# A two-layer decoder trunk on one core: the first products of each stage in a fixed order, the statistics product at tile 1, the Silu table loaded behind the affines

## The chip, the cores and the metric

The kernel runs on one core of one Trainium2 chip. A core has a tensor engine (PE in the profile, with its weight loads as PEld), a vector engine (DVE), a scalar engine (ACT), GpSimd (POOL) and a sync engine (SP) that issues most transfers. Each engine takes its instructions in the order in which they stand in its own queue; between engines they wait for semaphores. Products are summed in PSUM, in banks of 128 partitions by 512 columns; all other data lies in SBUF. The metric is device time in microseconds, the median of several runs. Times inside a profile count from the first instruction.

## The reference

One sequence of 512 positions with 1024 channels runs through two layers. Layer 0 mixes tokens with stick-breaking attention, layer 1 with a diagonal state-space layer; behind each mixer stands a gated feed-forward stage with a causal convolution of width 3. Each of these four stages starts with a root-mean-square norm that a conditioning vector scales and shifts. Cut to what matters here:

```python
def rms_norm(x, g):
    xf = x.astype(jnp.float32)
    y = xf * lax.rsqrt(jnp.mean(xf * xf, axis=-1, keepdims=True) + EPS)
    return (y * g.astype(jnp.float32)).astype(x.dtype)

def modulate(h, shift, scale):
    return h * (1 + scale[:, None, :]) + shift[:, None, :]

def conv_ffn(h, w_up, conv_w, conv_b, w_down):
    up = h @ w_up
    up = lax.conv_general_dilated(
        up, conv_w[:, None, :], window_strides=(1,), padding=[(CONV_W - 1, 0)],
        dimension_numbers=('NWC', 'WIO', 'NWC'), feature_group_count=2 * D_FF) + conv_b
    gate, val = jnp.split(up, 2, axis=-1)
    return (jax.nn.silu(gate) * val) @ w_down

# in reference(), for each layer i
        x = x + g1[:, None, :] * y
        h = modulate(rms_norm(x, norm_ffn[i]), sh2, sc2)
        x = x + g2[:, None, :] * conv_ffn(h, w_up[i], conv_w[i], conv_b[i], w_down[i])
```

## The kernel before

**Layout and precision.** Activations lie with channels on partitions: `x` is eight tiles of 128 channels by 512 positions, and so is the normed `h`. Every operand of a product is split into a high and a low part, made by ACT (the rounded copy) and DVE (the difference): `hH`, `hL` for `h`, and names ending in `_h`, `_l` for weights. A product of one weight tile and one tile of `h` is then three: high by high, high weight by low `h`, low weight by high `h`. The function `mm3` (L170 to L177) issues them in this order. Eight tiles make one output of 128 channels by 512 positions in one PSUM bank.

**Heads.** A stage's *head* is its first four outputs, computed while the norm in front of the stage is still being made: `head_mm` (L324 to L345) in both feed-forward stages (products `up`, of units 0 and 1, each a gate and a value) and in the state-space layer (products `u`, four of eight). The norm's statistics come in two halves of 256 positions. The first half's product stands in the stage before; the second half's is issued inside the head by `rstd_stat`, at a place that `HEADS` gives. Its result lets `norm_tile` (L304 on) make the second half of `h`: for each tile one multiplication on DVE (`nt`), two affines on ACT (`hH`, and `nt` again in place of a full-precision copy), one subtraction on DVE (`hL`). The head goes through tiles 0 to 5 for the first 256 positions, tiles 0 to 5 for the second 256, and tiles 6 and 7 for all 512, and multiplies each tile with all four weights.

**What sets the order.** A scheduler orders each engine's queue by its own estimate of times. `pe_pin` keeps an instruction in the order of the program, and `behind_head` and `follow` issue one behind given others. In the head before, only some products are pinned: those of tile 0 and the statistics product. The rest is left to the scheduler, which may put products of the next unit among them.

**Buffers.** PSUM's main pool has six banks, handed out in turn. In a feed-forward stage the head holds four of them and unit 2 the next two. In layer 0 the result `gm` of the gate of units 2 and up takes a main bank as well (units 0 and 1 use another pool), and unit 3 follows. Split weights go round in five buffers of each kind (`NW`), raw weights in three; two of the head's four weights lie in such buffers and two in their own. The loop over `HEADW` issues the loads and splits of the next five weights (the products of units 2 and 3 and the first of unit 4), each behind a given tile's affines.

**Behind the head.** `unit_out` (L467 on) takes a unit out of PSUM: `conv` evicts with ACT (`ca`, L462) and adds two taps on DVE (L464), ACT makes Silu of the gate (L474), DVE multiplies gate and value (`gm`), ACT and DVE split the result into `gH` and `gL`. The first Silu needs another function table on ACT than the norm before it, so an ACT_TABLE_LOAD stands there. In layer 0, DVE, ACT and POOL also prepare tables for the state-space layer in between (L1020 to L1078 and others). In the state-space layer `u_out` (L1297 to L1300) copies a finished `u` to memory and reads it back in another layout; the first block's products `pv` (L1291) wait for it.

Of the kernel before, what the change touches and what calls it, by code (L numbers as in the profile page):

```python
# [8 lines left out]
F32 = mybir.dt.float32  # L9
# [3 lines left out]
AF = mybir.ActivationFunctionType  # L13
# [4 lines left out]
P = 128  # L18
T = 512
D = 1024  # L20
KD = D // P
# [11 lines left out]
STATK = 0  # L33
STATN = 2
HEADK = 6
HEADS = (1, 2)
HEADW = (4, 8, 11, 13, 13)
UPRE = 12
NACC = 6
NIDLE = (5, 2, 0, 9, 0)  # L40
# [48 lines left out]
def _trunk(ctx, tc, I, out, tap):  # L89
# [15 lines left out]
    def pe_pin(ins):  # L105
        tc.keep_in_program_order(ins)
# [64 lines left out]
    def mm3(ps, lhs, rhs, start, stop, pinned=False):  # L171
        (ah, al), (bh, bl) = lhs, rhs
        ins = PE.matmul(ps, ah, bh, start=start, stop=False)  # L173
        if pinned:
            tc.keep_in_program_order(ins)
        PE.matmul(ps, ah, bl, start=False, stop=False)  # L176
        PE.matmul(ps, al, bh, start=False, stop=stop)  # L177
# [148 lines left out]
    def head_mm(R, h, a, b, hd):  # L326
        pin["head"] = []
        todo = [(k, HALF[0]) for k in range(HEADK)] + [(k, HALF[1]) for k in range(HEADK)] + [(k, FULL) for k in range(HEADK, KD)]
        made = 0
        for n, (k, cr) in enumerate(todo):  # L330

            while made < (min(n + 3, HEADK) if cr == HALF[0] else n + 1):
                norm_tile(h, todo[made][0], R["bc"], a, b, todo[made][1])
                made += 1
            for q, (w, ps) in enumerate(hd):
                if cr == HALF[0] and (k, q) == HEADS:
                    rstd_stat(R, HALF[1], True)
                if n:
                    mm3(ps[:, cr], wk(w, k), (h[0][k][:, cr], h[1][k][:, cr]), k == 0 and cr.start == 0, k == KD - 1)
                else:  # L340
                    for half in range(2):
                        pe_pin(PE.matmul(ps[:, cr], wk(w, k)[half], h[0][k][:, cr], start=not half, stop=False))
            if not n:
                for w, ps in hd:
                    pe_pin(PE.matmul(ps[:, cr], wk(w, k)[0], h[1][k][:, cr], start=False, stop=False))  # L345

    @contextmanager
    def behind_head(pins=None):
# [80 lines left out]
    def ffn(l, R, prep=None, last=None, hook=lambda: None):  # L429
# [4 lines left out]
        with ExitStack() as fc:  # L434
# [61 lines left out]
            for gi, gn in enumerate(GROUPS):  # L496
                gs = []
                i = i0
                if gi == 2:
                    hook()  # L500
                if gi == 0:
                    hx, ws = pin["hw"]
                    hd = [(q, s, ws[2 * q + s], bank(name=f"up{l}_{q}_{s}")) for q in range(2) for s in range(2)]
                    head_mm(R, h, a, b, [q[2:] for q in hd])
                    hx.close()
                    for q in range(len(HEADW)):
                        with behind_head(pin["head"][HEADW[q]]):
                            split_next(q > 2)
                    if not l:
                        bg(2, False, hold=behind_head)  # L510
                    pin["prep"] = [pin["split"]]
                    for q in range(2):
                        gs.append(unit_out(q, q, [hd[2 * q + s][3] for s in range(2)]))
                    i = 2
                    step = prep(fc) if prep else (lambda: None)
                for i in range(i, i0 + gn):
                    av = []
                    for s in range(2):
                        w, ps = take(), bank(name=f"up{l}_{i}_{s}")
                        for k in range(KD):  # L520
                            mm3(ps, wk(w, k), (h[0][k], h[1][k]), k == 0, k == KD - 1)
                        av.append(ps)
                    skip = [i == 2]

                    def nxt():
                        if not skip or not skip.pop():
                            split_next()

                    gs.append(unit_out(i, i - i0, av, nxt))
                    if l or (4, 0, 0)[gi] <= i - i0 < (8, 2, 6)[gi]:  # L530
                        bg(BGU if l else 1, lined=True)
                    pace(11.0)

                def after():
                    if l == 0 and gi < 2:
                        bg(1, lined=True)
                    pace(5.4)

                head = None
                if gi == 2 and prep:  # L540
                    while step():
                        pass
                    head = [I["w_in"][bi * P:(bi + 1) * P, :] for bi in range(4)], "win"
                R2 = out_proj(lambda mt: I["w_down"][(l * KD + mt) * P:(l * KD + mt + 1) * P, i0 * P:(i0 + gn) * P], gs, mcol(l, 5, 0),
                         acc2 if gi == 2 else None, f"dn{l}_{gi}_", tail=TAIL + (FINT if last else 0), n=gn * P, after=after, last=last if gi == 2 else None, head=head,
                         getw=lambda mt: take(), step=split_next)
                i0 += gn
# [956 lines left out]
    R = ssm(R)  # L1504
# [156 lines left out]
```

## Time and profile before

| | |
|---|---|
| Median of 3 runs | 1162.76 us (1162.4 to 1164.23) |
| The profiled execution | 1162.41 us |
| Its span, first to last instruction | 1160.6 us |
| Mean granted TensorE clock | 0.997 |
| Head of layer 0's feed-forward stage | from 252.90 us |
| Head of the state-space layer | from 626.1 us |
| Head of layer 1's feed-forward stage | from 789.0 us |

Busy shares are of the span. The span in 40 slices, with the busy share of each engine in tenths:

```profile
PE   9999999999999999999999999999999999999997
DVE  7869989576998577687867598787598378744655
ACT  7656577455552244313347477547443144422443
POOL 1001110000589799879800000000000000000003
PEclk9999999999999999999999999999999999999999
```

PE is busy in every slice. The other lines that carry the argument stand in the prediction. A row of a timeline reads: start, duration, engine, line of the kernel, operation, what it writes and reads, sizes and count; in brackets stand idle time of the engine before it and what ended that.

### The profile page before, as it was taken

How to read it: one execution, taken by the hardware profiler on the slowest of the kernel's cores; microseconds unless marked ns; L12 is line 12 of the kernel's file. 1: busy time of each engine (PE TensorE's matmuls, PEld its weight loads, DVE VectorE, ACT ScalarE, POOL GpSimd, SP SyncE). 2: the span in 40 equal slices, each digit the busy share in tenths (PEclk: the TensorE clock that was granted, in tenths of full speed). 3: DMA queues.
4: the chain of work that ended last, by engine and by line, in shares of the span. 5: the costliest groups of instructions: out<-in, count | busy, mean ns of one | idle time of the engine just before them, and what ended most of it. 6: DMA issues, size and time to landing. Idle time of an engine off the chain costs nothing.

```text
span 1160.6 us, 16497 instructions
## 1 busy us (share of the span) xinstructions
PE 1149.5 (99%) x6212; PEld 960.4 (83%) x6212; DVE 854.4 (74%) x1273; ACT 563.1 (49%) x896; POOL 274.5 (24%) x279
## 2 busy tenths in 40 slices
PE   9999999999999999999999999999999999999997
PEld 7888777797888888888889888889888888888887
DVE  7869989576998577687867598787598378744655
ACT  7656577455552244313347477547443144422443
POOL 1001110000589799879800000000000000000003
PEclk9999999999999999999999999999999999999999
DMA  9875464323166668697766598461176357432222
GB/s 347 283 261 173 167 212 147 130 91 110 55 221 219 206 233 252 196 315 237 236 202 231 175 348 279 168 212 55 38 232 220 109 161 197 128 114 74 94 69 73
DMA packets 87777, 211.01 MB, mean 182 GB/s; under 512 B 15505, under 2 KB 33809, under 8 KB 87698
## 3 DMA queue, kind: packets, MB, share of 16 engines
q1 hardware_dynamic: 78994, 192.65, 50.6%
q0 software_dynamic: 4544, 16.26, 4.2%
q10 hardware_dynamic: 4160, 1.05, 0.4%
q8 instruction: 49, 0.80, 0.3%
q14 instruction: 30, 0.25, 0.1%
HBM read 188.68 MB, written 21.24 MB: 181 GB/s over the span
## 4 chain that ended last, share of the span: by engine, by line
PE 95%; DVE 2%; ACT 1%; POOL 1%; issue 1%; POOLq 0%; ACTq 0%
PE up L173 13%; PE up L177 13%; PE up L176 13%; PE dn L173 7%; PE dn L176 7%; PE dn L177 7%; PE o L838 2%; PE t L822 2%; PE glu L173 1%; PE wo L173 1%; PE py L1291 1%; PE u L173 1%; PE wo L176 1%; PE wo L177 1%; PE wos L177 1%; PE wos L176 1%
## 5 line engine op out<-in xcount | busy, mean ns | idle before, releaser
L173 PE MATMUL up<-hH,up_h 128*128 128x512 f32 x640 | 250.7, 392 | 2.4 <-DVE e L1028 2.4
L177 PE MATMUL up<-hH,up_l 128*128 128x512 f32 x640 | 249.8, 390 | 0.2 <-DVE up_l L168 0.2
L176 PE MATMUL up<-hL,up_h 128*128 128x512 f32 x640 | 249.9, 390 | 0.0
L464 DVE SCALAR_TENSOR_TENSOR ca<-up,small,ca 128x511 f32<-128x511 f32 (+1 forms) x176 | 131.5, 747 | 103.9 <-ACT ca L462 101.1
L173 PE MATMUL dn<-gH,dn_h 128*128 128x512 f32 (+1 forms) x394 | 144.5, 368 | 0.0
L176 PE MATMUL dn<-gL,dn_h 128*128 128x512 f32 (+1 forms) x394 | 144.5, 367 | 0.0
L177 PE MATMUL dn<-gH,dn_l 128*128 128x512 f32 (+1 forms) x394 | 144.4, 366 | 0.0
L173 PEld LDWEIGHTS up<-hH,up_h 128*128 128x128 f32 x640 | 120.4, 188 | 28.7 <-issue 3.6
L177 PEld LDWEIGHTS up<-hH,up_l 128*128 128x128 f32 x640 | 120.5, 188 | 25.7 <-DVE up_l L168 0.8
L176 PEld LDWEIGHTS up<-hL,up_h 128*128 128x128 f32 x640 | 120.6, 188 | 24.8
L168 DVE TENSOR_TENSOR up_l<-up_r,up_h 128x1024 fp32r<-128x1024 f32 x80 | 116.6, 1459 | 24.8 <-ACT up_h L167 20.9
L462 ACT ACTIVATE ca<-up,small 128x512 f32<-128x512 f32 x88 | 68.1, 774 | 132.9 <-PE up L177 132.9
L167 ACT ACTIVATE up_h<-up_r 128x1024 fp32r<-128x1024 f32 x80 | 84.0, 1053 | 93.8 <-PE dn L176 59.1
L204 DVE SCALAR_TENSOR_TENSOR wg<-wg,cact 128x1024 f32<-128x1024 f32 x96 | 120.7, 1276 | 6.0 <-DMA wg<-in_w_modT_dram 6.0
L1533 POOL TENSOR_SCALAR xa<-x,Anorm_out 128x256 f32<-128x256 f32 x7 | 5.7, 817 | 459.6 <-ACT dn_h L167 446.9
L360 DVE SCALAR_TENSOR_TENSOR x<-dn,mod,x 128x512 f32<-128x512 f32 (+1 forms) x55 | 37.4, 681 | 70.7 <-PE dn L177 70.3
L173 PEld LDWEIGHTS dn<-gH,dn_h 128*128 128x128 f32 x394 | 74.3, 189 | 12.8 <-issue 0.6
L177 PEld LDWEIGHTS dn<-gH,dn_l 128*128 128x128 f32 x394 | 74.3, 189 | 12.2
L176 PEld LDWEIGHTS dn<-gL,dn_h 128*128 128x128 f32 x394 | 74.3, 189 | 12.1
L167 ACT ACTIVATE dn_h<-dn_r 128x1024 fp32r<-128x1024 f32 (+1 forms) x48 | 46.5, 980 | 47.7 <-PE dn L176 37.7
L168 DVE TENSOR_TENSOR dn_l<-dn_r,dn_h 128x1024 fp32r<-128x1024 f32 (+1 forms) x48 | 59.6, 1242 | 0.7 <-ACT dn_h L167 0.5
L480 ACT ACTIVATE gH<-gm 128x512 fp32r<-128x512 f32 x44 | 27.1, 616 | 68.0 <-DVE gm L476 68.0
(370 smaller groups left out, 2297.0 us busy)
## 6 DMA issues: line engine op xcount, KB each, us to landing
up_r<-in_w_up_dram SPq DMA_DIRECT2D x80, 512.0 KB
wg<-in_w_modT_dram SPq DMA_DIRECT2D x74, 512.0 KB
dn_r<-in_w_down_dram SPq DMA_DIRECT2D x32, 512.0 KB
wg<-in_w_modT_dram POOLq DMA_DIRECT2D x22, 512.0 KB, 4.6
wgs<-in_w_modT_dram SPq DMA_DIRECT2D x16, 512.0 KB
dn_r<-in_w_down_dram SPq DMA_DIRECT2D x16, 384.0 KB
wv_r<-in_w_v_dram SPq DMA_DIRECT2D x8, 512.0 KB
wk_r<-in_w_qk_dram SPq DMA_DIRECT2D x8, 512.0 KB
```

The costliest lines, as they stand in the source:

```text
L167: order("S", lambda: S.activation(wh[:, :n], raw[:, :n], AF.Copy))
L168: pin["split"] = order("V", lambda: V.tensor_tensor(wl[:, :n], raw[:, :n], wh[:, :n].bitcast(F32), ALU.subtract))
L173: ins = PE.matmul(ps, ah, bh, start=start, stop=False)
L176: PE.matmul(ps, ah, bl, start=False, stop=False)
L177: PE.matmul(ps, al, bh, start=False, stop=stop)
L204: mul = lambda: V.scalar_tensor_tensor(w, w, 1.0, cact, ALU.mult, ALU.mult, accum_out=raw[:, col:col + 1])
L360: add = lambda: V.scalar_tensor_tensor(xs, pv, gate, xs, ALU.mult, ALU.add)
L462: follow("S", lambda: S.activation(ca, ps, AF.Identity, bias=small[:, cb:cb + 1], scale=tapw[2]))
L464: follow("V", lambda: V.scalar_tensor_tensor(ca[:, q:], ps[:, :T - q], tapw[2 - q], ca[:, q:], ALU.mult, ALU.add))
L480: follow("S", lambda: S.activation(gh, m, AF.Copy))
L822: pe_pin(PE.transpose(pt[:, c:c + P], wts[pr][h2][i][:, j * P:(j + 1) * P], ident))
L838: pe_pin(PE.matmul(po[pr][h2 * HD:(h2 + 1) * HD, j * P:], vn[:, j, hd:hd + HD], src, start=j == 0, stop=j == 3))
```

## The change

Four edits:

- In `head_mm`, all products are pinned, in a new order: for each tile first the products with its high part (high and low weight, for all four outputs), then those with its low part. What was left to the scheduler is now written out, so the next unit's products stand behind the head.
- `HEADS` is a tile: the second statistics product stands between the high and the low products of tile 1 in the first half. Before, it was ahead of output 2 of tile 1, and the scheduler moved it in the feed-forward stages, where the unpinned products came ahead of it or behind it.
- `HEADW` has four entries, so the loop splits four weights and not five, and none of them in the recorded order that `lined=True` gave the fourth and fifth. The fifth comes in `unit_out` of unit 2, where the call that was skipped before is now made. The first product of unit 2 is pinned.
- A one-column Silu (`warms`) is issued behind the last affines, so the table load stands there.

```diff
-HEADS = (1, 2)
-HEADW = (4, 8, 11, 13, 13)
+HEADS = 1
+HEADW = (4, 8, 11, 13)
...
-            for q, (w, ps) in enumerate(hd):
-                if cr == HALF[0] and (k, q) == HEADS:
-                    rstd_stat(R, HALF[1], True)
-                if n:
-                    mm3(ps[:, cr], wk(w, k), (h[0][k][:, cr], h[1][k][:, cr]), k == 0 and cr.start == 0, k == KD - 1)
-                else:
-                    for half in range(2):
-                        pe_pin(PE.matmul(ps[:, cr], wk(w, k)[half], h[0][k][:, cr], start=not half, stop=False))
-            if not n:
-                for w, ps in hd:
-                    pe_pin(PE.matmul(ps[:, cr], wk(w, k)[0], h[1][k][:, cr], start=False, stop=False))
+            def prod(ps, half, low):
+                return pe_pin(PE.matmul(ps[:, cr], wk(w, k)[half], h[low][k][:, cr], start=k == 0 and cr.start == 0 and half + low == 0, stop=k == KD - 1 and low == 1))
+
+            for w, ps in hd:
+                for half in range(2):
+                    prod(ps, half, 0)
+            if cr == HALF[0] and k == HEADS:
+                rstd_stat(R, HALF[1], True)
+            for w, ps in hd:
+                prod(ps, 0, 1)
...
-                            split_next(q > 2)
+                            split_next(False)
                     if not l:
                         bg(2, False, hold=behind_head)
+                    warm = np_.tile([P, 64], F32, tag="warm", bufs=1, name="warms")[:, 0:1]
+                    with behind_head():
+                        S.activation(warm, ones[:, 0:1], AF.Silu)
...
-                            mm3(ps, wk(w, k), (h[0][k], h[1][k]), k == 0, k == KD - 1)
+                            mm3(ps, wk(w, k), (h[0][k], h[1][k]), k == 0, k == KD - 1, i == 2 and not k)
                         av.append(ps)
-                    skip = [i == 2]
-
-                    def nxt():
-                        if not skip or not skip.pop():
-                            split_next()
-
-                    gs.append(unit_out(i, i - i0, av, nxt))
+                    gs.append(unit_out(i, i - i0, av, split_next))
```

How the queues change, at three places. The first is PE in the head of layer 0's feed-forward stage, where the second half of tile 0 begins. `up0_0_0` to `up0_1_1` are the four outputs of the head (layer, unit, gate or value), `upo0` to `upo3` their weights, `up0_2_0` the gate of unit 2. Before:

```order
L173 MATMUL up0_0_0_2586<-hH0_2566,upo0_h_2362 128x256
L173 MATMUL up0_0_1_2587<-hH0_2566,upo1_h_2368 128x256
L173 MATMUL up0_1_0_2588<-hH0_2566,upo2_h_2374 128x256
L173 MATMUL up0_1_1_2589<-hH0_2566,upo3_h_2380 128x256
L173 MATMUL up0_2_0_2918<-hH0_2566,up0_2_0_h_2850 128x512
L176 MATMUL up0_0_0_2586<-hL0_2574,upo0_h_2362 128x256
L177 MATMUL up0_0_0_2586<-hH0_2566,upo0_l_2363 128x256
L176 MATMUL up0_0_1_2587<-hL0_2574,upo1_h_2368 128x256
```

And in the changed kernel, from the same place in the queue:

```order
L336 MATMUL up0_0_0_2586<-hH0_2566,upo0_h_2362 128x256
L336 MATMUL up0_0_0_2586<-hH0_2566,upo0_l_2363 128x256
L336 MATMUL up0_0_1_2587<-hH0_2566,upo1_h_2368 128x256
L336 MATMUL up0_0_1_2587<-hH0_2566,upo1_l_2369 128x256
L336 MATMUL up0_1_0_2588<-hH0_2566,upo2_h_2374 128x256
L336 MATMUL up0_1_0_2588<-hH0_2566,upo2_l_2375 128x256
L336 MATMUL up0_1_1_2589<-hH0_2566,upo3_h_2380 128x256
L336 MATMUL up0_1_1_2589<-hH0_2566,upo3_l_2381 128x256
L336 MATMUL up0_0_0_2586<-hL0_2574,upo0_h_2362 128x256
L336 MATMUL up0_0_1_2587<-hL0_2574,upo1_h_2368 128x256
```

The product of unit 2, and 18 more like it in the rest of this head, now stand behind the head; the first product with the low part is the ninth, not the sixth. The statistics product, in the first half of the head, moves 20 products forward here and in layer 1; in the state-space layer it keeps its place.

The second place is ACT behind the affines of the same head: `ca0` is the eviction of a gate, `ca1` of a value, `up0_3_1_h` and `up0_4_0_h` are high parts of the fourth and the fifth weight. Before:

```order
L317 ACTIVATE nt2_2831<-nt1_2830,mod_110,Anorm_ffn0_2564 128x512
L167 ACTIVATE up0_3_1_h_2868<-up0_3_1_r_2867 128x1024
L167 ACTIVATE up0_4_0_h_2874<-up0_4_0_r_2873 128x1024
L462 ACTIVATE ca0_2885<-up0_0_0_2586,small_86 128x512
L474 ACT_TABLE_LOAD
L474 ACTIVATE gm_2889<-ca0_2885 128x512
L462 ACTIVATE ca1_2891<-up0_0_1_2587,small_86 128x512
L480 ACTIVATE gH0_2896<-gm_2889 128x512
```

In the changed kernel:

```order
L317 ACTIVATE nt2_2831<-nt1_2830,mod_110,Anorm_ffn0_2564 128x512
L512 ACT_TABLE_LOAD
L512 ACTIVATE warms_2879<-ones_103 128x1
L461 ACTIVATE ca0_2881<-up0_0_0_2586,small_86 128x512
L167 ACTIVATE up0_3_1_h_2868<-up0_3_1_r_2867 128x1024
L473 ACTIVATE gm_2885<-ca0_2881 128x512
L461 ACTIVATE ca1_2887<-up0_0_1_2587,small_86 128x512
L479 ACTIVATE gH0_2892<-gm_2885 128x512
L461 ACTIVATE ca0_2896<-up0_1_0_2588,small_86 128x512
L473 ACTIVATE gm_2900<-ca0_2896 128x512
L461 ACTIVATE ca1_2902<-up0_1_1_2589,small_86 128x512
L479 ACTIVATE gH1_2907<-gm_2900 128x512
```

The table load stands ahead of the first eviction, the fourth weight's split behind it, and the fifth's has gone further back, behind the eviction of unit 2's gate. DVE's halves of these splits move with them. In layer 1 the same happens.

The third place is PE at the end of the state-space layer's head: `u0` to `u3` are its outputs, `win0` to `win3` their weights. Before:

```order
L176 MATMUL u0_6046<-hL7_6015,win0_h_5831 128x512
L177 MATMUL u0_6046<-hH7_6007,win0_l_5832 128x512
L176 MATMUL u1_6047<-hL7_6015,win1_h_5837 128x512
L177 MATMUL u1_6047<-hH7_6007,win1_l_5838 128x512
L176 MATMUL u2_6048<-hL7_6015,win2_h_5843 128x512
L177 MATMUL u2_6048<-hH7_6007,win2_l_5844 128x512
L176 MATMUL u3_6049<-hL7_6015,win3_h_5849 128x512
L177 MATMUL u3_6049<-hH7_6007,win3_l_5850 128x512
```

In the changed kernel:

```order
L336 MATMUL u3_6051<-hH7_6009,win3_h_5851 128x512
L336 MATMUL u3_6051<-hH7_6009,win3_l_5852 128x512
L336 MATMUL u0_6048<-hL7_6017,win0_h_5833 128x512
L336 MATMUL u1_6049<-hL7_6017,win1_h_5839 128x512
L336 MATMUL u2_6050<-hL7_6017,win2_h_5845 128x512
L336 MATMUL u3_6051<-hL7_6017,win3_h_5851 128x512
```

The last product of `u0` is the fourth from the end, where it was the seventh. Besides, the scheduler moves three things by itself: in the state-space layer one load of a weight on SP's queue goes behind four other loads; in layer 1's first down group six products with the last slice come 21 products earlier; in layer 0 the table preparation on POOL and DVE is interleaved a little differently.

## The prediction

> **What bounds the kernel now.** I read the page's busy times first, then the list of who waited for whom on the tensor engine (PE), then the timeline at the one place where that list has something to give.
>
> ```profile
> span 1160.6 us, 16497 instructions
> PE 1149.5 (99%) x6212; PEld 960.4 (83%) x6212; DVE 854.4 (74%) x1273; ACT 563.1 (49%) x896; POOL 274.5 (24%) x279
> PE 95%; DVE 2%; ACT 1%; POOL 1%; issue 1%; POOLq 0%; ACTq 0%
> ...
> PE up L173 <- DVE e L1028: 2.4, 1, 2.4
> PE up L177 <- DVE up_l L168: 0.2, 1, 0.2
> ```
>
> PE is the path: 99% busy, and 95% of the chain that ended last. The last two rows are from its waits (us in total, times, longest). The change adds and removes no product, so it can gain only PE time that is not products at full speed, and it loses what PE must newly wait. Apart from the first 16 us, where the change does nothing, the list has one wait of 2.4 us and one of 0.2 us. PE's own timeline and its clock show what the larger one costs:
>
> ```profile
> 286.84 0.39 PE L177 MATMUL up<-hH,up_l 128*128 128x512 f32 x1
> 289.65 0.47 PE L173 MATMUL up<-hH,up_h 128*128 128x512 f32 x1 [2.43 <-DVE e L1028]
> ...
> 291.20 0.63 PE L173 MATMUL up<-hH,up_h 128*128 128x512 f32 x1
> 291.62 0.63 PE L176 MATMUL up<-hL,up_h 128*128 128x512 f32 x1
> ...
> 294.53 0.39 PE L177 MATMUL up<-hH,up_l 128*128 128x512 f32 x1
> 294.75 0.39 PE L173 MATMUL up<-hH,up_h 128*128 128x512 f32 x1
> ...
> 289.60:291.00 1.40, 1.35 (x6) 1.00 0.00 0
> 291.00:294.20 3.20, 3.20 (x10) 0.50 0.00 0
> ```
>
> The last two rows give stretches: PE's busy time, its instructions, then the granted clock. A 512-column product normally starts 0.22 to 0.23 us after the one before (294.53 to 294.75). After the wait, with the clock at 0.50, the step is 0.42 (291.20 to 291.62). From the product at 286.84 to that at 294.53 there are 15 steps; at 0.2275 they need 3.41 us, and they took 7.69. **The stall costs 4.28 us**: 2.6 for the wait, 1.7 for the clock behind it.
>
> Why PE waited: the six PSUM banks go round in the order of allocation. Unit 2's `gm` takes the bank of product (0, gate), so the first product of unit 3 takes that of (0, value), which comes free when the vector engine (DVE) has done its second tap. The scalar engine (ACT) and DVE came late there:
>
> ```profile
> 271.33 0.81 ACT L317 ACTIVATE nt<-nt,mod,Anorm_ffn 128x512 f32<-128x512 f32 x1
> 279.97 2.01 ACT L167 ACTIVATE up_h<-up_r 128x1024 fp32r<-128x1024 f32 x2 [7.82 <-PE up L176]
> 281.89 0.76 ACT L462 ACTIVATE ca<-up,small 128x512 f32<-128x512 f32 x1
> 285.35 1.28 ACT L474 ACT_TABLE_LOAD   x1 [2.70 <-DVE ca L464]
> 287.18 0.76 ACT L462 ACTIVATE ca<-up,small 128x512 f32<-128x512 f32 x1
> 298.38 0.78 ACT L462 ACTIVATE ca<-up,small 128x512 f32<-128x512 f32 x1
> ...
> 288.76 0.75 DVE L464 SCALAR_TENSOR_TENSOR ca<-up,small,ca 128x510 f32<-128x510 f32 x1
> ```
>
> ACT is done with h at 272.14, then stands 7.8 us before two weight splits that need buffers of the head, and only behind them, at 281.89, evicts unit 0. The bank is free at 289.51, the end of the last row; PE goes on at 289.65.
>
> **The change part by part.** (1) The head's products end earlier. Before, 19 products of unit 2 stood among them by the program's order; at 0.23 each, 4.4 us, these go behind. The head starts at 252.90 and its statistics product at 257.66 (rows below), 40 products later, so a product of 256 columns takes 0.119. It holds 144 of these, 24 of 512 columns at 0.23, and the statistics product with at most 0.59: 252.90 + 17.14 + 5.52 + 0.59 = 276.2. Product (0, gate) is done four low products from the end, near 275.6, so its eviction starts then, 6.3 us before 281.89, if nothing stands ahead of it on ACT. In the new order nothing does: the two splits are behind it, and the table load (1.28) falls in the idle time from 272.14 on. That idle time is its cover; without it the load would cost ACT 1.28 again. From eviction to free bank took 289.51 - 281.89 = 7.62; less the load, plus one split that now stands in the chain (up to 1.23 on DVE), it stays 7.6, so the bank is free by 283.2. PE, with as many products ahead of it as before, wants it at 286.84 + 0.23 = 287.07. Margin 4 us: **the stall goes, -4.28**. Late next is the split of the fifth weight, moved behind unit 2's gate eviction: that stood 298.38 - 281.89 = 16.5 behind the first, so near 292, and its two halves (1.0 on ACT, 1.2 on DVE, two taps of 0.75 ahead) are done near 295; PE wants them two product groups after 287.07, at 298. Margin 3 us.
>
> (2) The head itself, in the two feed-forward layers. What covers PE there against late affines was the 19 products; now nothing does.
>
> ```profile
> 252.90 0.28 PE L342 MATMUL up<-hH,upo_h 128*128 128x256 f32 x1
> 257.66 0.59 PE L284 MATMUL stat<-acc,ones 128*128 128x256 f32 x2
> 261.88 0.64 PE L173 MATMUL up<-hH,upo_h 128*128 128x256 f32 x4
> ...
> 254.41 0.43 DVE L252 TENSOR_TENSOR acc<-acc,sq 128x256 f32<-128x256 f32 x1
> 256.95 1.23 DVE L168 TENSOR_TENSOR up_l<-up_r,up_h 128x1024 fp32r<-128x1024 f32 x1 [0.53 <-ACT up_h L167]
> 258.80 0.42 DVE L289 SCALAR_TENSOR_TENSOR ntw<-dg 128x256 f32<-128x256 f32 x1 [0.29 <-ACT dg L288]
> ...
> 260.64 0.60 ACT L315 ACTIVATE hH<-nt,mod,Anorm_ffn 128x256 fp32r<-128x256 f32 x1 [1.87 <-DVE nt L308]
> 261.63 0.59 ACT L315 ACTIVATE hH<-nt,mod,Anorm_ffn 128x256 fp32r<-128x256 f32 x1
> 262.73 0.58 ACT L315 ACTIVATE hH<-nt,mod,Anorm_ffn 128x256 fp32r<-128x256 f32 x1
> 263.83 1.05 ACT L167 ACTIVATE up_h<-up_r 128x1024 fp32r<-128x1024 f32 x1
> ```
>
> The statistics product moves 20 products forward, from 257.66 to 255.3; its accumulator is ready at 254.84, 0.4 ahead, so I cost it at nothing (if the add slips by more, PE waits that much). It does not bring the second half 2.4 forward: DVE is in a weight split until 258.18, so the chain starts at 258.1 instead of 258.8, and one subtraction moved into it takes half of that back; the first high part is ready near 260.9. PE comes to it at 261.88 as before. Then PE eats a tile in 12 x 0.119 = 1.43; ACT makes one in 1.10 (261.63 to 262.73) and has two splits of about 1.0 within six tiles: 8.6 for both. The margin stays near 1.0: no wait. The low parts gain: four more products stand ahead of them. The state-space layer has such a head without a filler already, since its next products were pinned behind it:
>
> ```profile
> 632.47 0.59 ACT L315 ACTIVATE hH<-nt,mod,Anorm_mix 128x256 fp32r<-128x256 f32 x1
> ...
> 635.58 0.64 PE L173 MATMUL u<-hH,win_h 128*128 128x256 f32 x4
> ```
>
> ACT writes the first high part of the second half by 633.1, PE comes to it at 635.6 and waits nowhere in that head; but the margin is 2.5, not 1.0. So the term is **0, with bounds 0 and +2** (the margin missed by 1 us in each of the two layers).
>
> (3) In that state-space head the order within a tile costs: u0's last product was the seventh from the end, now it is the fourth, 3 x 0.23 = 0.7 later. u0 goes through memory and back:
>
> ```profile
> 648.15 0.40 PE L177 MATMUL u<-hH,win_l 128*128 128x512 f32 x1
> ...
> 658.03 0.39 PE L1291 MATMUL pv<-u,pB 128*64 128x64 f32 x6
> ...
> 654.22 1.69 SPq L1300 DMA_DIRECT2D u<-sU  x2
> ...
> ball<-in_b_re_dram POOLq DMA_DIRECT2D x1, 256.0 KB, 3.7
> ```
>
> Issued at 654.22 and used at 658.03, it has 3.8 us, and the quickest landing that the page lists for 256 KB is 3.7: no slack is to be seen. Behind pv0 stand, pinned, all further products, so PE waits for it. Between 0 and 0.7 I take **+0.6**. One weight load on SP's queue moves behind four other loads there; its products come several blocks of work later, and were it wanted at once it would cost one landing, 3.7. I take nothing.
>
> (4) Layer 1: the 0.2 us wait is at a weight split that came late by the same chain (0.59 from one start to the next, below, for 0.23). There the evictions start some 6 us earlier too: **-0.36**. The first down group's last slices now come 21 products sooner: 42 products after 878.10, at 887.7, and the last one is written at 886.7. Margin 1.0, nothing.
>
> ```profile
> 839.73 0.39 PE L176 MATMUL up<-hL,up_h 128*128 128x512 f32 x1
> 840.32 0.50 PE L177 MATMUL up<-hH,up_l 128*128 128x512 f32 x1 [0.21 <-DVE up_l L168]
> ...
> 878.10 0.39 PE L173 MATMUL dn<-gH,dn_h 128*128 128x512 f32 x1
> ...
> 885.99 0.69 DVE L481 TENSOR_TENSOR gL<-gm,gH 128x512 fp32r<-128x512 f32 x1
> ```
>
> **Sum**: -4.28 + 0 + 0.6 - 0.36 = -4.0. The profiled execution took 1162.41, span 1160.6 and 1.8 around it; it becomes 1158.4. It lies 0.35 under the median of the runs shown, 1162.76, so I say **1158.5**.
>
> **The rivals.** *The clock does not follow the wait.* The half clock lasts from about 291 to 294.5 and I put it down to the wait just before it; it is the only such place between the start and the end. If it were its own event, only 2.6 of the 4.28 goes: 1158.5 + 1.7 = 1160.2. Against it: it begins 1.4 us behind the wait and comes nowhere else. The Trainium skill, "TensorE: Matmul & The Clock Gate", section "What's actually happening", says that the clock is halved after at least one idle window of about 3.4 us; read strictly, an idle time of 2.43 us would not do it, the half clock would have another cause and stay, and the sum would be this rival's. The trace speaks against that reading, since the half clock stands right behind those 2.43 us.
>
> *The change does not do what it says*, or the stall only moves: the affines of the second half are late by 1 to 2 us in both heads, with nothing to fill. 1158.5 + 2 x 1.0 to 2 x 2.0: 1160.5 to 1162.5, no measurable change above 1160.4. For it: the margin of 1.0 is worked out, not seen. Against it: it rests on the same instructions on ACT and DVE at the same times as now.
>
> *Slower*: the same place, but far enough that PE's clock halves as well, 1.7 a time as priced above. With both heads waiting 1.6 us or more beyond the margin, 1158.5 + 2 x (1.6 + 1.7) = 1165.1, and slower from there: 1166. It decides where the first high part of the second half comes at 263.5 instead of 260.9. Against it: nothing on ACT or DVE moves by that much there.
>
> **How the numbers follow.** Forecast 70%, clock stays 9%, stall moves 14%, slower 7%. The forecast's own terms reach from 1157.8 (no wait for u0) to 1159.5 (a part of the +2); I open it at the bottom by the spread of the runs, to 1157.2, and upwards through the clock rival and into the third, to 1161.3, which leaves about 2 in 10 out. A measurement of this kernel can tell 0.2%, 2.3 us, from no change; the bound is 1160.4. Faster by more: the forecast, the clock rival and little else, 78%. Within: 15%. Slower: 7%.
>
> **What would show it.** Right: no PE wait on unit 3's first product, no half clock after the first 5 us until the end, the table load right behind the last affine, unit 0's eviction near 3.4 us after it; a wait of about 0.6 on pv0. Wrong: a PE wait on `up` for ACT or DVE within a head (2), a PE wait on `stat` for DVE (2), a bank still freed after 287 (1), half clock without a wait (rival one).

## The result and the profile after

| | before | changed |
|---|---|---|
| Median, first series | 1162.65 us (6 runs, 1162.4 to 1164.9) | 1157.97 us (6 runs, 1156.95 to 1160.62) |
| Ratio, first series | | 0.9957, 95% interval 0.9944 to 0.997 |
| Median, second series | 1162.35 us (9 runs) | 1157.1 us (5 runs, 1156.75 to 1159.08) |
| Ratio, second series | | 0.9958, 95% interval 0.9945 to 0.997 |

The changed kernel is faster by 4.7 to 5.3 us, 0.4%. Its first profile ran in 1158.33 us. Below are three lines of its page (span, busy times, the chain that ended last by engine):

```profile
span 1156.6 us, 16495 instructions
...
PE 1147.8 (99%) x6212; PEld 961.1 (83%) x6212; DVE 856.2 (74%) x1273; ACT 564.5 (49%) x898; POOL 275.0 (24%) x279
...
PE 98%; POOL 1%; DMA 0%; ACT 0%; issue 0%; SPq 0%; DVE 0%; POOLq 0%; ACTq 0%
```

And all of its PE waits (engine, line, what it waited for, us in total, times, longest):

```profile
PE spare L1475 <- DVE ones L129: 1.1, 1, 1.1
PE v L659 <- ACT hH L672: 0.8, 1, 0.8
PE t L818 <- ACT wT L821: 0.3, 1, 0.3
```

DVE's 2% of the chain are gone and PE has 98% of it. No wait on `up` is left; the three that stay lie ahead of layer 0's head. (The one on `t`, behind the start and the same before and after, is missing from the prediction's reading of the list.) The timeline at the old place of the stall, PE first (the first product of unit 3 is the one at 288.28), then ACT and DVE behind the head:

```profile
288.05 0.39 PE L177 MATMUL up<-hH,up_l 128*128 128x512 f32 x1
288.28 0.39 PE L173 MATMUL up<-hH,up_h 128*128 128x512 f32 x1
...
272.31 0.82 ACT L317 ACTIVATE nt<-nt,mod,Anorm_ffn 128x512 f32<-128x512 f32 x1
273.14 1.28 ACT L512 ACT_TABLE_LOAD   x1
...
276.88 0.78 ACT L461 ACTIVATE ca<-up,small 128x512 f32<-128x512 f32 x1 [2.24 <-PE up L336]
277.56 1.05 ACT L167 ACTIVATE up_h<-up_r 128x1024 fp32r<-128x1024 f32 x1
...
279.86 0.77 ACT L461 ACTIVATE ca<-up,small 128x512 f32<-128x512 f32 x1
...
281.55 0.74 DVE L463 SCALAR_TENSOR_TENSOR ca<-up,small,ca 128x510 f32<-128x510 f32 x1
```

The bank of product (0, value) is free at 282.29, the end of the last row, 6.0 us before PE takes it; before, PE had to wait for it and began unit 3 2.6 us late. From the first eviction to the free bank it took 5.41 (276.88 to 282.29), where it had taken 7.62.

Where the time went is read from the first product of each stretch. The change can do nothing before layer 0's head, but the start differs from run to run, so the second profile of the changed kernel (span 1155.3 us) stands beside the first:

| Stretch, us | before | changed, first | changed, second |
|---|---|---|---|
| Start to the first `v` product | 16.28 | 17.96 | 16.34 |
| to the head of layer 0 | 236.62 | 236.43 | 236.60 |
| to the first product of unit 3 | 36.75 | 33.89 | 33.88 |
| to the state-space head | 336.45 | 334.72 | 334.88 |
| to the first `pv` | 31.93 | 31.70 | 31.73 |
| to the head of layer 1 | 130.96 | 130.96 | 131.00 |
| to the first down product | 89.11 | 88.34 | 88.34 |
| to the end | 282.53 | 282.55 | 282.55 |

Between before and the second profile, with nearly the same start, the sum is -5.31. The start is PE's clock: the stretch behind 12.7 us runs at 0.50 in the first profile and at 1.00 in the second, and the first `v` product comes 1.6 us later. The view of stretches gives the stretch, its length, PE's busy time and instructions, the granted clock, DMA share and GB/s. The first profile:

```profile
12.72:16.13 3.41, 3.41 (x18) 0.50 1.03 412
```

The second:

```profile
12.70:16.10 3.40, 3.13 (x22) 1.00 1.03 413
```

So two runs of the same kernel differ by 1.5 us at the start alone; the stretches of the profiles are the finer measure, and the experiments are read by them.

### The profile page after: what moved, and what is told of

The parts are those of the page before. It is cut to its first block, busy times and chain, and to the rows that moved or that the text cites. A ratio compares the mean times of both kernels' runs of the same rounds, so it can differ in the third digit from the quotient of the medians.

```text
span 1156.6 us, 16495 instructions
## 1 busy us (share of the span) xinstructions
PE 1147.8 (99%) x6212; PEld 961.1 (83%) x6212; DVE 856.2 (74%) x1273; ACT 564.5 (49%) x898; POOL 275.0 (24%) x279
## 4 chain that ended last, share of the span: by engine, by line
PE 98%; POOL 1%; DMA 0%; ACT 0%; issue 0%; SPq 0%; DVE 0%; POOLq 0%; ACTq 0%
PE up L173 13%; PE up L176 13%; PE up L177 13%; PE dn L173 7%; PE dn L176 7%; PE dn L177 7%; PE up L336 4%; PE u L336 2%; PE o L834 2%; PE t L818 2%; PE glu L173 1%; PE wo L173 1%; PE py L1287 1%; PE wo L176 1%; PE wo L177 1%; PE wos L177 1%
```

## The experiments

**The two halves of the change alone.** The first has the heads of before and the new splits and table load; its diff against before is shown. The second has the new heads and the old splits and table load: the same lines the other way round, against the changed kernel.

```diff
-HEADW = (4, 8, 11, 13, 13)
+HEADW = (4, 8, 11, 13)
...
-                            split_next(q > 2)
+                            split_next(False)
+                    warm = np_.tile([P, 64], F32, tag="warm", bufs=1, name="warms")[:, 0:1]
+                    with behind_head():
+                        S.activation(warm, ones[:, 0:1], AF.Silu)
...
-                    skip = [i == 2]
-
-                    def nxt():
-                        if not skip or not skip.pop():
-                            split_next()
-
-                    gs.append(unit_out(i, i - i0, av, nxt))
+                    gs.append(unit_out(i, i - i0, av, split_next))
```

> The kernel before with the second half of the change alone: four splits and none recorded, the fifth weight split behind unit 2's gate eviction, the Silu table behind the affines. The heads and the order on PE in layer 0 stay as before, with unit 2's 19 products among the head's. Theory (either half is enough): before, product (0, gate) had its last product at 278.84, and its eviction waited until 281.89 for two splits that need buffers of the head. Without them it starts near 279.2; from there to the free bank 5.4 us, as in the changed kernel, where it also has no table load in it: 284.6, 2.5 ahead of the 287.07 at which PE comes. The stall goes with its half clock, -4.3, and layer 1's late split, -0.4: 1158.0. No gain within the heads. Rival (the pinned heads are what removes it): the bank is free after 287, a PE wait of 1 us or more on unit 3's first product stays, 1160 to 1162.5.

> The changed kernel with the first half of the change alone: the heads pinned in the new order and the statistics product at tile 1, but five splits, of which the fourth and fifth stand ahead of the first eviction, and the Silu table behind it, as before. Theory (either half is enough): the head ends about 4.4 us of filler earlier, but the two splits (2.0 us on the scalar engine) still need its buffers, so the first eviction starts 3.4 earlier than before, at 278.5 on the clock of before; 7.6 from there to the free bank, as before: 286.1, 1.0 ahead of 287.07. The stall goes, barely: -4.3, and -0.25 in each of three heads: 1157.6 to 1158. Rival (the splits and the table load are what stalls): PE waits 1 to 2.5 us on unit 3's first product, the clock halves behind it or not, 1159 to 1162.

Splits and Silu alone: 1160.35 us (8 runs), ratio 0.9973 (0.9962 to 0.9984). Heads alone: 1156.95 us (5 runs), 0.9947 (0.9934 to 0.9959). Timeline of the splits alone: eviction, last tap, and PE with unit 3's first product at 288.50:

```profile
280.72 0.78 ACT L462 ACTIVATE ca<-up,small 128x512 f32<-128x512 f32 x1 [5.61 <-PE up L177]
285.38 0.74 DVE L464 SCALAR_TENSOR_TENSOR ca<-up,small,ca 128x510 f32<-128x510 f32 x1
288.28 0.39 PE L177 MATMUL up<-hH,up_l 128*128 128x512 f32 x1
288.50 0.39 PE L173 MATMUL up<-hH,up_h 128*128 128x512 f32 x1
```

And of the heads alone, with unit 3's first product at 287.00:

```profile
276.06 2.01 ACT L167 ACTIVATE up_h<-up_r 128x1024 fp32r<-128x1024 f32 x2 [4.18 <-PE up L336]
277.98 0.76 ACT L461 ACTIVATE ca<-up,small 128x512 f32<-128x512 f32 x1
281.44 1.28 ACT L473 ACT_TABLE_LOAD   x1 [2.70 <-DVE ca L463]
...
284.85 0.75 DVE L463 SCALAR_TENSOR_TENSOR ca<-up,small,ca 128x510 f32<-128x510 f32 x1
...
286.77 0.39 PE L177 MATMUL up<-hH,up_l 128*128 128x512 f32 x1
287.00 0.39 PE L173 MATMUL up<-hH,up_h 128*128 128x512 f32 x1
```

In both, PE goes on without a gap and no half clock follows: **either half takes the stall away**. The bank is free 2.4 us ahead of PE with the splits alone (286.12 against 288.50) and 1.4 with the heads alone (285.60 against 287.00). The heads alone have every stretch of the changed kernel to within 0.2 us; the other half adds only slack to it.

The splits alone fell short of the expected 1158.0. Their heads stay at the length of before, and a new wait came 200 us later. It stands in the list of waits:

```profile
PE dn L176 <- DVE gL L481: 0.8, 1, 0.8
```

The scalar engine at that place, in the timeline:

```profile
483.98 1.06 ACT L167 ACTIVATE dn_h<-dn_r 128x1024 fp32r<-128x1024 f32 x1 [4.22 <-DMA dn_r<-in_w_down_dram]
```

A down weight landed late, its split stood ahead of `gL` on DVE, and PE waited for that. From layer 0's head to the state-space head it is 370.52 us, against 368.61 in the changed kernel. Of the 1.91 more, 0.28 lie in the head, 1.17 at this wait and the product behind it, 0.36 at a product `pk` near 420 and 0.10 at a statistics product near 621.

> The kernel with the splits and the Silu table alone once more. Its first profile lost the stall as expected (-4.3) but came out 1.5 us longer in layer 0's second and third group: a down weight's load stood at 477.0 on SP's queue behind transfers of the state-space tables, some 5 us later than in the other kernels against PE, its split held up gL on the vector engine, and PE waited 0.8 on dn. Theory (it is set by this kernel's order of the table preparation): the wait on dn comes again, 0.5 to 1.0, and the segment from layer 0's head to the state-space head is again 370 to 371: 1159 to 1161. Rival (it is a chance of the transfers in that run): no wait on dn, segment 368.9 to 369.2, 1158 to 1159.

The second profile has the same wait at 0.2 us and 369.60 for the stretch; 1159.84 us (10 runs), 0.9972 (0.9961 to 0.9984). It comes again, by an amount that varies: between the theory and its rival. What goes with it: the GpSimd multiplications of the state-space tables start 46.9 us after layer 0's head in both profiles, as before the change (46.7), while they start at 42.6 with the heads alone and at 43.0 in the changed kernel. With the splits alone PE runs 4.3 us ahead and the table work does not follow. That its transfers therefore meet the down weights is argued from these times; no run separates it.

**The table load.** The changed kernel without the one-column Silu.

```diff
-                    warm = np_.tile([P, 64], F32, tag="warm", bufs=1, name="warms")[:, 0:1]
-                    with behind_head():
-                        S.activation(warm, ones[:, 0:1], AF.Silu)
```

> The changed kernel without the one-column Silu, so that the table load stands behind the first eviction again. Theory (the bank now has 4 us or more to spare, so 1.28 us more on the scalar engine are covered): no change against the changed kernel, 1158.0, no PE wait on up; unit 0's Silu 0.5 to 1.3 later. Rival (the table load ahead is needed): a PE wait on up in layer 0 or 1, 0.5 to 3 us, 1158.5 to 1161.

1157.4 us (5 runs), 0.9949 (0.9936 to 0.9963): no change. Timeline: table load, last tap and, 370 us later, the first `pv`:

```profile
278.20 1.28 ACT L473 ACT_TABLE_LOAD   x1 [0.70 <-DVE ca L463]
...
281.68 0.74 DVE L463 SCALAR_TENSOR_TENSOR ca<-up,small,ca 128x510 f32<-128x510 f32 x1
...
654.15 0.36 PE L1284 MATMUL pv<-u,pB 128*64 128x64 f32 x5 [0.41 <-issue]
```

From eviction (275.78) to free bank (282.42) it is 6.64, 1.23 more than in the changed kernel: the load costs nearly its whole length there, and 4.8 us of slack hide it. The wait on `pv` was not there in the changed kernel, though the state-space layer's queues are the same in both; it is taken up below.

**The order within a tile.** Heads pinned, but one output after the other; the mark that ends an output's sum moves to the product that is now its last.

```diff
...
-            for w, ps in hd:
-                for half in range(2):
-                    prod(ps, half, 0)
-            if cr == HALF[0] and k == HEADS:
-                rstd_stat(R, HALF[1], True)
-            for w, ps in hd:
-                prod(ps, 0, 1)
+            for q, (w, ps) in enumerate(hd):
+                if cr == HALF[0] and k == HEADS and q == 2:
+                    rstd_stat(R, HALF[1], True)
+                for half, low in ((0, 0), (0, 1), (1, 0)):
+                    prod(ps, half, low)
```

> The changed kernel, heads pinned, but within each tile in the order of before (high by high, low h, low weight, for one output after the other), the statistics product ahead of output 2 of tile 1. Theory (the high-first order covers the low parts of h, which in the layer 0 head are written 0.2 us ahead of where this order would use them at tiles 0 and 3 and 0.25 us behind it at tile 6): PE loses 0.25 us in each of the three heads, the gain that the changed kernel's heads showed over those of before, 1158.7. Rival one (the order within a tile is worth nothing): 1158.0. Rival two (the low parts are late at every tile): some 0.3 us at each of eight tiles, 2 us a head, 1163. u0's last product also comes 0.7 earlier in the state-space head, which is worth nothing if u0 is not waited for.

1158.8 us (5 runs), 0.9963 (0.9951 to 0.9976). The times alone cannot tell it from the changed kernel; the stretches can. From a head's first product to the 212th behind it: 32.94 in layer 0, against 32.52 in the changed kernel and 32.80 with the heads of before; 32.82 in layer 1, against 32.58 and 32.83. So pinning alone gains nothing in the heads; **the order does, 0.42 in layer 0 and 0.24 in layer 1**. In layer 0, 0.30 of it lies at the first product with the low part of tile 6: it starts 0.42 behind the one before it, and the next another 0.34 later, each for 0.23. In the state-space head the low part of tile 0 comes late in this order, as the timeline shows:

```profile
624.40 0.39 PE L336 MATMUL u<-hL,win_h 128*128 128x256 f32 x1 [0.67 <-DVE hL L321]
```

(The heads of before had tile 0 in the high-first order already, so they did not have this wait.)

**The statistics product later**, in the changed kernel, at tile 2 (shown) and at tile 3.

```diff
-HEADS = 1
+HEADS = 2
```

> The changed kernel with the statistics product at tile 2 instead of tile 1 (1.42 us later). In the changed kernel the first high part of the second half of h is written at 262.21 and PE comes to it at 263.31, 1.09 ahead, and tile 6's at 270.84 against 271.79, 0.95 ahead; the state-space head has 2.5. Theory (the margins are real and the chain behind the product shifts with it): 0.3 to 0.5 us of wait in each feed-forward head, none in the state-space one, +0.6 to +1.0: 1158.7. Rival (the vector engine's split that stands ahead of the chain sets its start, not the product): no wait, 1158.0.

> The changed kernel with the statistics product at tile 3 (2.85 us later than at tile 1). Theory: the chain shifts by all of it, so PE waits 2.85 - 1.09 = 1.8 on up in each feed-forward head, and up to 0.35 on u in the state-space head: +3.6 to +4.0, 1161.8, and if an idle time of 1.8 already halves the clock, up to 1.7 more each time, 1165. Rival (the chain does not follow the product): under 1 us in all, 1158.5 to 1159.

Tile 2: 1158.59 us (5 runs), 0.9962 (0.995 to 0.9975). Tile 3: 1159.94 us (6 runs), 0.9968 (0.9956 to 0.998). The theory of both expectations fell, in the feed-forward heads: no wait on `up` is listed. With tile 2 layer 0's head is as long as in the changed kernel and layer 1's 0.17 longer; with tile 3 each is about 0.14 longer. (The two new waits of the profile with tile 2 lie elsewhere, 0.3 at a statistics product near 618 and 0.6 on `pv`; no run shows that tile 2 causes them.) The rival of the second expectation, under 1 us in all, fell as well, by what the state-space layer adds. The vector engine shows why the heads hardly move. Timeline of the changed kernel (split of a weight, first step of the chain, first high part of the second half, PE's first use of it):

```profile
258.44 1.23 DVE L168 TENSOR_TENSOR up_l<-up_r,up_h 128x1024 fp32r<-128x1024 f32 x1 [0.52 <-ACT up_h L167]
...
259.58 0.42 DVE L289 SCALAR_TENSOR_TENSOR ntw<-dg 128x256 f32<-128x256 f32 x1
...
261.62 0.60 ACT L315 ACTIVATE hH<-nt,mod,Anorm_ffn 128x256 fp32r<-128x256 f32 x1 [1.88 <-DVE nt L308]
...
263.31 0.28 PE L336 MATMUL up<-hH,upo_h 128*128 128x256 f32 x1
```

The same rows with the product at tile 3:

```profile
258.69 1.23 DVE L168 TENSOR_TENSOR up_l<-up_r,up_h 128x1024 fp32r<-128x1024 f32 x1 [0.53 <-ACT up_h L167]
...
260.98 0.42 DVE L289 SCALAR_TENSOR_TENSOR ntw<-dg 128x256 f32<-128x256 f32 x1 [0.72 <-ACT dg L288]
...
262.81 0.60 ACT L315 ACTIVATE hH<-nt,mod,Anorm_ffn 128x256 fp32r<-128x256 f32 x1 [1.87 <-DVE nt L308]
...
263.57 0.29 PE L336 MATMUL up<-hH,upo_h 128*128 128x256 f32 x1
```

The two heads start at 254.39 and 254.65. Counted from there, the high part is begun at 7.23 and 8.16: the product moved by 2.8 us and the chain by 0.93, since in the changed kernel a weight split holds DVE until 259.67 anyway. The high part was done 1.09 before its use (262.22 against 263.31) and is now done 0.16 before it. In the state-space layer tile 3 has waits of 0.5 on `u` and 1.1 on `pv`.

**Does the half clock follow the wait?** In the kernel before, four or eight products (n) are added in the idle time ahead of unit 3. They repeat the last product of unit 2's value, so that its contribution counts five or nine times: these two serve to see the clock and do not compute the reference.

```diff
-                            mm3(ps, wk(w, k), (h[0][k], h[1][k]), k == 0, k == KD - 1)
+                            mm3(ps, wk(w, k), (h[0][k], h[1][k]), k == 0, k == KD - 1 and (l, i, s) != (0, 2, 1))
+                        for q in range(n if (l, i, s) == (0, 2, 1) else 0):
+                            PE.matmul(ps, wk(w, KD - 1)[1], h[0][KD - 1], start=False, stop=q == n - 1)
```

> The kernel before with the last, low product of unit 2's value (up0_2_1) issued four times more, so that its contribution counts five times: 0.9 us of products in what was an idle time of 2.6 us, ahead of unit 3's first product, which still cannot start before 289.65. Theory (the half clock behind the stall follows from PE's idle time): with 1.7 us idle left the half clock becomes rarer or goes, 1161.3 to 1163; the wait on up is 1.5. Rival (the half clock is an event of its own): time and half clock as before, 1163.

> The same with eight more, which count nine times: 1.8 us of products in the idle time, 0.8 us of it left. Theory (the half clock follows from the idle time): no half clock behind the stall, 1163.0 - 1.7 = 1161.3, a wait on up of 0.6 to 0.8. Rival (an event of its own): the half clock stays near 291 and the time at 1163. Second rival (the clock only needs a wait, however short): as the first in time.

Four more: 1162.84 us (11 runs), 0.9997 (0.9989 to 1.0006). Eight more: 1161.96 us (11 runs), 0.9994 (0.9985 to 1.0003). In time neither can be told from the kernel before (1162.99, 22 runs); the clock shows more. Stretches, columns as above: the kernel before, at the stall and behind it:

```profile
287.60:291.00 3.40, 1.35 (x6) 1.00 0.00 1
291.00:294.40 3.40, 3.40 (x10) 0.50 0.00 0
```

With four more, the same two stretches:

```profile
289.15:292.55 3.40, 1.88 (x9) 1.00 0.00 0
292.55:295.96 3.41, 3.41 (x17) 1.00 0.00 0
```

With eight more:

```profile
289.58:293.00 3.42, 2.80 (x13) 1.00 0.00 0
293.00:296.41 3.41, 3.41 (x17) 1.00 0.00 0
```

The unit's bank comes free at the same time, and **with 1.5 us of wait instead of 2.4 the half clock is gone**, with 0.6 too. The other runs, without profiles, agree: each has its mean granted clock on record. A half clock of 3.41 us takes 0.0015 off it, and the one at the very end takes more (1.5 to 4.8 us of it lie in the span in the 14 profiles), so a mean of 0.999 leaves room for the end's alone, as an estimate from these figures. Of the kernel before, 9 of 56 runs have 0.999; with four more products 6 of 11, with eight 7 of 11. So the half clock here follows PE's idle time, and the rivals that it is an event of its own, or that any wait is enough, fall; but it did not follow the stall in every run of the kernel before. Of the 1.7 only 0.86 is gained (unit 3 to the state-space head 335.59 and 335.61, for 336.45), since PE now runs into the next late bank, as the list of waits of the kernel with four more shows:

```profile
PE up L173 <- DVE mag L1033: 0.5, 1, 0.5
```

**The round trip of `u0`, and a faster version?** The changed kernel again; then with the last tile of each head in the order of one output after the other, so that `u0` ends earlier; then that on the heads alone.

```diff
             for w, ps in hd:
                 for half in range(2):
                     prod(ps, half, 0)
+                if k == KD - 1:
+                    prod(ps, 0, 1)
...
-            for w, ps in hd:
+            for w, ps in hd if k < KD - 1 else ():
                 prod(ps, 0, 1)
```

> The changed kernel once more, for a second profile and beside the next two. All theories: 1157.5 to 1158.5; every segment as in the first profile, but for the start, which is 1.5 us longer where one window of half clock falls into it, and for u0's way through memory: PE's wait on pv was 0 in the changed kernel and in the one with the heads alone, 0.4 to 1.1 in three other kernels with the same order in the state-space head. Theory (the round trip has no slack in the new order, so the wait varies from run to run): 0 to 0.7 here. Rival (it is set by the kernel): 0 again.

> The changed kernel with the last tile of each head in the order of one output after the other (high, low weight, low h), so that u0's last product is the third of the last twelve and not the ninth, 1.4 us earlier; unit 0's gate ends earlier by as much. Theory (term of the round trip): u0 is back 1.4 us earlier, no wait on pv in any profile, 0 to 0.7 gained in a run that had the wait: 1157.3 to 1158.0. Rival (the round trip is set by other transfers on its queue): a wait on pv stays possible, same time as the changed kernel. No wait within the heads, since the low part of tile 7 is written 0.7 ahead.

> The same last tile, with the pinned heads alone (five splits, two of them and no table load ahead of the first eviction): the candidate for the fastest. Theory: as the kernel with the heads alone, 1156.9 to 1157.5, no wait on up and none on pv. Rival (in the changed kernel's heads the splits matter in other runs than the profiled one): 1158 or more, a wait on up.

1157.1 us (5 runs), 1157.17 us (5 runs, 0.9955, 0.9943 to 0.9968) and 1157.45 us (5 runs, 0.9956, 0.9943 to 0.997). None of the three waits more than 0.1 us for `u0`, and none is faster than the changed kernel. Over all profiles: where `u0`'s last product is the ninth of the last twelve, PE waited for `pv` 0, 0, 0, 0.4, 0.6 and 1.1 us (the last with a late head); where it stands earlier, 0 in eight of eight. The profile names nothing that ends this wait (its row says "issue"). But counted from the issue of `u0`'s write to memory, the first `pv` comes at 8.13 to 8.16 us in the three profiles without the wait and at 8.62, 8.81 and 9.33 in the others; less their waits that is 8.20 to 8.22. PE is there at the same point each time, and the way through memory is what varies.

## Why the prediction was right, and where it was not

**The stall (-4.28) was right.** It measures 2.6 of wait and 1.6 to 1.7 of half clock, in two rows of the table of stretches: -2.86, less 0.28 for the head, and -1.57 to -1.73. That is its price in the profiled run; at least 9 of the 56 runs above had no half clock behind the stall. The eviction started at 275.4 on the clock of before, as worked out (275.6). The chain behind it was put at 7.6 and took 5.41, because the split that I added to it costs nothing (ACT does it while it waits for DVE's taps), and because the fifth weight's split no longer holds DVE ahead of the taps. So the margin was 6 and not 4. What the prediction did not see is that the change removes the stall twice.

**The heads (0, bounds 0 to +2) were mis-sized, on the side that the bounds left out.** The margin of 1.0 for the second half measured 1.09, and the reason given for it, the weight split on DVE, is what the later statistics product showed. But each head became shorter: -0.28, -0.2 and -0.25, -0.7 in all. I had counted cover lost with the 19 products; that the low parts gain cover I had said, but gave it no price.

**The round trip (+0.6) was 0 in both profiles of the changed kernel.** That its slack is small was right: with the same order it was waited for in three of six profiles. It is a cost of some runs, and I entered nearly its upper end as if it came in all. The 3.7 that I set against its 3.8 was the landing of another transfer of this size: with the statistics product at tile 2, `u0`'s read was issued at 651.02 and used at 654.22, 3.20 later. What varies most is the stretch ahead of it, from the issue of the write to that of the read: 4.2 to 5.7 in these six profiles. I had not counted it.

**Layer 1 (-0.36)** measured -0.77 less 0.25 for its head, -0.52. The late split cost more than the one step that I read: in the timeline of before, the product behind it (840.32) is followed after 0.34 us and not 0.23:

```profile
840.66 0.40 PE L173 MATMUL up<-hH,up_h 128*128 128x512 f32 x1
```

The splits and Silu alone have the same -0.52 there. The first down group's slices caused no wait.

From layer 0's head to the end it is -5.57 in the first profile and -5.35 in the second, where I said -4.0. The first profile still came out at 1158.33 beside the 1158.4 of the sum, because the slower start added 1.5; that agreement is luck. The medians, 1157.97 and 1157.1, lie 0.5 and 1.4 under the forecast, inside the range or just below it. Of the rivals, the clock's fell with the added products; the one of late affines fell: no head waits for ACT or DVE in the changed kernel, nor with the statistics product at tile 2.

## What to carry to other kernels

When a bank or buffer comes late, list everything between the last reader and its release on each engine; if two of these can be moved, either may be enough, and the second buys slack, not time. A moved producer shifts its chain only as far as the engine behind it was free, so read what that engine does at that time before pricing the move. And a stage that starts earlier need not take its helpers along: with the splits alone the table work kept its old times, and a weight came late 200 us behind. Look there too, though the link between the two is argued here.

## What the runs showed of the hardware

The granted clock changes on a grid. In the trace's clock records the half clock lasts from 291.007 to 294.420 in the kernel before, 84 steps of 3.413 us after the first full clock at 4.287, and from 12.720 to 16.134 in the first profile of the changed kernel, two steps after 5.894. The Trainium skill, "TensorE: Matmul & The Clock Gate", section "What's actually happening", calls the window free-running, with 3413 ns; the records agree. The Trainium skill, in the same section, puts the half clock after at least one idle window. Here a window idle for 60% (1.35 of 3.40 busy) was enough, and one idle for 45% (1.88 of 3.40) was not; the measurement decides. The ends of the kernels, with products of 128 columns and of one, point to the same place: the last window that holds products is busy for 1.85 us with eight more products, and the clock stays full behind it; it is busy for 1.77 with one output after the other, and half clock follows.

But busy time in the trace is not all that the clock goes by. Where the grid lies at the start is worth 1.5 us by itself: of 14 profiles, six have a half clock near 13 us and their first `v` product at 17.8 to 18.2; eight have none and come to it at 16.1 to 16.7. In the six the first full clock comes at 5.8 to 6.7 us, in the eight at 4.1 to 5.0 or at 7.1 to 7.4. The window ahead of the half clock counts as at least 98% busy in all six, but it holds all 16 statistics products of one column each (10.63 to 12.44 in the first profile of the changed kernel). The view of PE alone, stretch and columns as above:

```profile
9.31:12.72 3.41, 3.36 (x26) 1.00 1.03 404
12.72:16.13 3.41, 3.41 (x18) 0.50 1.03 412
```

That such short products count for little is argued: the second profile of the splits alone has all 16 in one window too (10.81 to 14.22, 3.39 busy) and no half clock behind it.
